# A two-block transformer step in fp32: early sums on TensorE, chunks handed out by name, scan states on VectorE

## The chip, the cores and the metric

One core of a Trainium2 chip runs the whole program. The metric is device time in microseconds (us), the median of the runs shown. Engine names are those of the profile: PE is TensorE's matmul, PEld its weight load, DVE VectorE, ACT ScalarE, POOL GpSimd, and SP the engine that issues the large DMAs.

## What is computed

One sequence of 256 tokens with 1024 features, all in fp32, goes through two blocks.

```python
# block 1: nine vectors of 1024 from a condition, then three residual steps
mod = silu(cond) @ w_mod + b_mod                    # w_mod is 1024 x 9216
x += 0.5 * g1 * swiglu(modulate(rms_norm(x), sh1, sc1))          # ffn1
b_gate, c_gate, v, u = split(modulate(rms_norm(x), sh2, sc2) @ w_in)
y_conv = b_gate * conv3(c_gate * v)                 # causal, width 3
y_ssm  = y * sigmoid(y @ glu_w + glu_b),  y = gelu(S5(u))        # complex linear scan
x += g2 * (concat(rms_norm(y_conv), rms_norm(y_ssm)) @ w_out)    # mixer
x += 0.5 * g3 * swiglu(modulate(rms_norm(x), sh3, sc3))          # ffn2
x  = rms_norm(x, final_norm)
# block 2: gated linear attention, squared-relu MLP, differential attention, MLP
h += gla(rms_norm(h));   h += mlp0(rms_norm(h))
h += diff_attention(...); h += mlp1(rms_norm(h))
```

## The kernel before

**Weights.** Every large product is written as three matmuls of rounded fp32 parts (`mm3`, L248): activation high by weight high, activation low by weight high, activation high by weight low. All weights come as 1 MB chunks of 128 x 2048 values, in the one order that `schedule()` writes down. The class `Stream` moves them: `load` issues a DMA on SP into one of three stage buffers (L141); `prep` makes the high part on ACT (`wh`, L170) and the low part on DVE (`wl`, L172), in halves of 128 x 1024, into one of four slots (five after the mixer); `take` hands the next chunk of the order to its user and prepares as many more as slots are free, unless `ahead` limits that; `free` gives slots back. A chunk in `locked` stops `prep`, and with it all that stands behind it in the order, stage buffers and DMAs included.

**Order.** The program writes each engine's instructions in the order in which the Python code runs; each engine runs its queue in order. An instruction that waits holds all behind it on its engine.

**The modulation vectors.** A chunk of `w_mod` isn't prepared: its four calls per group g are summed on DVE (`macc`, L839 and L841, one operation for each half chunk), and `mod_reduce` sums over the partitions with matmuls of a single column against `ones` (L862) and adds the bias on DVE (L866, L868). Groups 0 and 1 give shift and scale of ffn1 and are needed before its first matmul; groups 2 to 6 are spread over ffn1, group 7 over the mixer, group 8 over ffn2.

**A gated ffn** takes 11 steps s of 256 hidden features: up and gate products (`up`), a hidden tile with its high and low part (`hidh` on ACT L276, `hidl` on DVE L277), and the product down into four banks (`acc`). The first three steps have no down product yet, and their hidden parts are split when the fourth begins. The last three down products are the `tail`: their parts are mixed by `turn` with the norm of the token half 0 (`post`, `evac`) and the first token-major products of the next layer (`turn`). `side1` runs after each step of ffn1: due modulation sums and `ssm.step(s)`.

**The S5 scan.** `ssm.powers()` works out powers of the complex decay on POOL (L586 to L698, and one DVE reciprocal at L666); `step(2..4)` transposes them on PE (`s_end`), `readout()` and `tables()` go on on POOL, `step(8..10)` make `s_lag`. In the mixer `turning(j)` runs the scan of one half of the channels, with nine operations on DVE and five on POOL (L1124 to L1137); `conv_a`, `conv_v`, `conv_b` are the convolution.

**GLA** makes the decay of its six levels with `level_e` (POOL, L1348 and L1349) and `across_e` (POOL), `exp` on ACT, and `level_x` on DVE (L1359, L1361); `diagonal` (L1385) and `level_mm` (L1370) are the small matmuls; `ks` (L1447) is q times k.

Of the kernel before, what the change touches and what calls it, by code (L numbers as in the profile page):

```python
# [18 lines left out]
S = 256  # L19
# [13 lines left out]
MODS_FFN1 = (2, 3, 4, 5, 6)  # L33
MODS_MIXER = (7,)
# [21 lines left out]
def schedule():  # L56

# [33 lines left out]

    mods(range(2))
    ffn("ffn1", MODS_FFN1, 1)
    md = [4 * g + c for g in MODS_MIXER for c in range(4)]
    for c in (6, 7, 2, 4, 0, 3, 5, 1):
        w("w_in", c)
        if c in (0, 3, 5, 1):
            w("w_mod", md.pop(0))
# [13 lines left out]
    mlp(0)  # L112
    for name, j in DIFF_ORDER:
        w(name, j)
    for c in range(4):
        w("b_out", c)
    mlp(1)
    return it


class Stream:
# [23 lines left out]
    def prep(self, upto, items=10 ** 9):  # L145

        nc = self.nc
        while self.n_prep < min(items, len(self.items)):
# [9 lines left out]
            else:  # L158
                n = st.shape[-1]
                if key in self.special:  # L160
                    pool, th, tl = self.special[key]
                    self.used.append(None)
                    h, lo = (pool.tile([128, n], F32R, name=nm, tag=tg, bufs=1) for nm, tg in (("wh", th), ("wl", tl)))
                else:
                    pool, slot = self.slots.pop(0)
                    self.used.append((pool, slot))
                    h, lo = (pool.tile([128, n], F32R, name=nm, tag="%s%d" % (nm, slot), bufs=1) for nm in ("wh", "wl"))
                cuts = [(c, min(n, c + 1024)) for c in range(0, n, 1024)]
# [4 lines left out]
                self.ready[self.n_slot] = key, (h, lo)  # L173
# [11 lines left out]
    def take(self, name, j=0, ahead=10 ** 9):  # L185
        i = self.n_take
        self.n_take += 1
        self.prep(i + 1 + ahead)
        key, W = self.ready.pop(i)
        assert key == (name, j), (key, name, j)  # L190
        return W


class Net:
# [195 lines left out]
    def tail(self, acc, last, first, post, order=None):  # L390
# [23 lines left out]
    def turn(self, tail, evac, chunks, use):  # L414
# [5 lines left out]
        if tail is None:  # L420
            evac(0)
            evac(1)
        else:
# [12 lines left out]
            S.prep(S.n_take + n_c)  # L436
            tail.post(1)
            if self.after_tail is not None:
                self.after_tail()
                self.after_tail = None  # L440
                S.prep(S.n_take + n_c)
        Ws = []
        for i in range(2):
            for c in range(n_c):
# [7 lines left out]
                if i == 0 and c == 1 and n_c > 2:  # L452
# [21 lines left out]
    def ffn(self, tail, evac, ups, dn, steps, gated, post, side=None, n_first=3):  # L474
# [48 lines left out]
        for s in range(n_first, steps):  # L523
            res = []
            for u in ups:
                ps = self.bank_u("up")
                self.feat(self.take(u, s), self.hT, v3(ps, 2))
# [36 lines left out]
class Ssm:  # L564


    def __init__(self, N, p):
# [136 lines left out]
    def step(self, s):  # L704
# [3 lines left out]
        if 2 <= s <= 4:  # L708
            for b in ((0, 1), (2, 3, 4), (5, 6, 7))[s - 2]:
# [73 lines left out]
def build(N):  # L783
# [64 lines left out]
    def mod_reduce(g, new_bank, later=False):  # L848
# [15 lines left out]
        def finish():  # L864
            col = modf[:, 2 * blk + kind, :]
            nc.vector.tensor_tensor(out=col, in0=bank[:, 0:KD], in1=sv["b_mod"][:, g, :], op=ADD)  # L866
            if kind == 1:
                nc.vector.scalar_tensor_tensor(out=col, in0=col, scalar=1.0, in1=(G_FFN1, G_MIX, G_FFN2)[blk], op0=ADD, op1=MUL)  # L868

        if later:  # L870
            return finish
        finish()
# [21 lines left out]
    N.pad("pad_slots", 64)  # L894
# [40 lines left out]
    def side1(s):  # L935
        mods_ready(True)
        ssm.step(s)

    tail_places("ffn1_w_down", 10, 0)
    tail = N.ffn(None, lambda i: N.evac_mod(pts[i], i, modf[:, 1, :], modf[:, 0, :], N.hT),  # L940
                 ("ffn1_w_gate", "ffn1_w_up"), "ffn1_w_down", 11, True, post_ffn1, side1, 1)
# [4 lines left out]
        convw=sv["conv_w"], glub=sv["glu_b"], onorm=sv["out_norms"], ones=ones, xns=xns, mods=mods_ready))  # L946
# [87 lines left out]
def mixer(N, tail, evac, ssm, c):  # L1034
# [3 lines left out]
    vt, gt, act = nc.vector.tensor_tensor, nc.gpsimd.tensor_tensor, nc.scalar.activation  # L1038
# [66 lines left out]
    conv_v(0, vps)  # L1105
# [12 lines left out]
    def turning(h, m):  # L1118
# [775 lines left out]
```

## Time and profile before

| | us |
|---|---|
| median of 3 runs (1244.81 to 1246.57) | 1246.31 |
| the profiled execution's own time | 1243.52 |
| its span in the trace | 1241.8 |
| PE busy | 1140.0 |
| DVE busy | 796.8 |
| ACT busy | 613.7 |
| POOL busy | 237.1 |

Busy time is the sum over the whole span, the same for stages that wait for different things; where an engine waits is read from the waits and from timelines of single stages. PE's clock is shown as the share that the throttle granted (1.00 is 2.4 GHz, 0.50 is 1.2 GHz). Weights read from memory are 227.87 MB in all.

### The profile page before, as it was taken

The numbers are of one execution on the slowest core, as the hardware profiler recorded it, in microseconds if no ns is written. First come the engines' busy times: TensorE is split into PE (matmuls) and PEld (weight loads), VectorE is DVE, ScalarE is ACT, GpSimd is POOL, SyncE is SP. The second block draws the span as 40 slices with busy tenths as digits, with TensorE's granted clock in tenths as the row PEclk, the third lists the DMA queues.
The fourth block names the chain that finished last, engine by engine and source line by source line (L and its number), as shares of the span: only waits on it lengthen the run. The fifth ranks groups of instructions, "written<-read, shape, count | busy, mean of one in ns | idle before, by whom it ended". The sixth has DMA issues, their size and how long they took to land.

```text
span 1241.8 us, 18751 instructions
## 1 busy us (share of the span) xinstructions
PE 1140.0 (92%) x7780; PEld 1055.1 (85%) x7780; DVE 796.8 (64%) x934; ACT 613.7 (49%) x941; POOL 237.1 (19%) x304
## 2 busy tenths in 40 slices
PE   2689999989788899999697998999999899999998
PEld 2678998979777889997697988999989898899997
DVE  7698788677877855454567656544468776545441
ACT  3444443564265544444473656555456665645541
POOL 8994399401400000000214100000000000000000
PEclk9989999999789999999897999999999899899999
DMA  8598788436243765563144255556435333455540
GB/s 319 205 326 310 270 321 325 149 136 238 94 177 137 281 235 180 174 233 105 68 149 158 73 182 204 177 200 203 170 136 200 107 136 119 173 193 180 180 157 34
DMA packets 33093, 230.13 MB, mean 185 GB/s; under 512 B 3680, under 2 KB 4064, under 8 KB 5872
## 3 DMA queue, kind: packets, MB, share of 16 engines
q1 hardware_dynamic: 31536, 224.05, 50.5%
q10 hardware_dynamic: 1472, 4.88, 1.1%
q8 instruction: 61, 1.00, 0.3%
q14 instruction: 24, 0.20, 0.0%
HBM read 227.87 MB, written 1.05 MB: 184 GB/s over the span
## 4 chain that ended last, share of the span: by engine, by line
PE 68%; DVE 15%; ACT 7%; POOL 4%; DMA 3%; issue 3%; ACTq 0%; DVEq 0%; POOLq 0%
PE acc L248 27%; PE up L248 25%; PE turn L248 8%; DVE wl L172 7%; PE kqv L248 2%; ACT wh L170 2%; POOL s_small L612 1%; PE xnT L335 1%; POOL s_small L615 1%; DVE macc L841 1%; PE lev L1370 1%; DMA stage<-in_w 1%; DMA stage<-in_a_in 1%; ACT s_lag L734 1%; PE glu L248 1%
## 5 line engine op out<-in xcount | busy, mean ns | idle before, releaser
L172 DVE TENSOR_TENSOR wl<-stage,wh 128x1024 fp32r<-128x1024 f32 x351 | 429.5, 1270 | 144.2 <-ACT wh L170 144.2
L170 ACT CAST wh<-stage 128x1024 fp32r<-128x1024 f32 x351 | 347.2, 1044 | 147.1 <-PE acc L248 37.5
L248 PE MATMUL up<-hTh,wh 128*128 128x256 f32 x1024 | 288.1, 281 | 0.2 <-ACT s_end L715 0.2
L248 PE MATMUL up<-hTl,wh 128*128 128x256 f32 x1024 | 287.0, 280 | 0.0
L248 PE MATMUL up<-hTh,wl 128*128 128x256 f32 x1024 | 286.9, 280 | 0.0
L248 PEld LDWEIGHTS up<-hTh,wl 128*128 128x128 f32 x1024 | 195.4, 191 | 0.0
L248 PEld LDWEIGHTS up<-hTh,wh 128*128 128x128 f32 x1024 | 192.5, 188 | 2.4 <-ACT s_end L715 0.5
L248 PEld LDWEIGHTS up<-hTl,wh 128*128 128x128 f32 x1024 | 192.4, 188 | 1.6 <-issue 0.2
L248 PE MATMUL acc<-wh,hidh 128*128 128x512 f32 x288 | 116.6, 405 | 10.7 <-ACT hidh L276 5.4
L248 PE MATMUL acc<-wh,hidl 128*128 128x512 f32 x288 | 116.1, 403 | 9.8 <-DVE hidl L277 9.5
L248 PE MATMUL acc<-wl,hidh 128*128 128x512 f32 x288 | 115.6, 401 | 1.7 <-DVE wl L172 1.7
L248 PE MATMUL turn<-wh,hTh 128*128 128x256 f32 x320 | 92.4, 289 | 10.2 <-ACT hTh L276 10.2
L248 PE MATMUL turn<-wl,hTh 128*128 128x256 f32 x320 | 91.6, 286 | 1.7 <-DVE wl L172 1.7
L248 PE MATMUL acc<-wh,macc 128*128 128x512 f32 x288 | 93.1, 391 | 0.0
L248 PE MATMUL turn<-wh,hTl 128*128 128x256 f32 x320 | 91.9, 287 | 0.0
L841 DVE SCALAR_TENSOR_TENSOR macc<-stage,cact,macc 128x1024 f32<-128x1024 f32 x63 | 85.5, 1358 | 4.1 <-DMA stage<-in_w_mod 2.6
L248 PEld LDWEIGHTS acc<-wh,hidl 128*128 128x128 f32 x288 | 55.9, 194 | 24.1 <-DVE hidl L277 11.6
L248 PEld LDWEIGHTS acc<-wh,hidh 128*128 128x128 f32 x288 | 55.9, 194 | 23.5 <-ACT hidh L276 6.3
L248 PEld LDWEIGHTS turn<-wh,hTh 128*128 128x128 f32 x320 | 62.5, 195 | 11.0 <-ACT hTh L276 10.8
L248 PEld LDWEIGHTS acc<-wl,hidh 128*128 128x128 f32 x288 | 55.9, 194 | 13.7 <-DVE wl L172 3.1
L248 PEld LDWEIGHTS turn<-wl,hTh 128*128 128x128 f32 x320 | 62.5, 195 | 2.1 <-DVE wl L172 1.9
L248 PEld LDWEIGHTS acc<-wh,macc 128*128 128x128 f32 x288 | 54.1, 188 | 11.0
(401 smaller groups left out, 2023.4 us busy)
## 6 DMA issues: line engine op xcount, KB each, us to landing
stage<-in_w SPq DMA_DIRECT2D x64, 1024.0 KB, 4.8
stage<-in_w_mod SPq DMA_DIRECT2D x36, 1024.0 KB, 5.0
stage<-in_ffn_w_gate SPq DMA_DIRECT2D x22, 1024.0 KB, 4.8
stage<-in_ffn_w_up SPq DMA_DIRECT2D x22, 1024.0 KB, 4.8
stage<-in_ffn_w_down SPq DMA_DIRECT2D x22, 1024.0 KB, 4.8
stage<-in_a_in SPq DMA_DIRECT2D x12, 1024.0 KB, 5.1
stage<-in_w_in SPq DMA_DIRECT2D x8, 1024.0 KB, 5.1
stage<-in_w_kv SPq DMA_DIRECT2D x8, 1024.0 KB, 4.9
```

What stands on the lines that cost most here:

```text
L170: nc.scalar.copy(out=h[:, b:e], in_=st[:, b:e])
L172: nc.vector.tensor_tensor(out=lo[:, b:e], in0=st[:, b:e], in1=h[:, b:e].bitcast(F32), op=SUB)
L248: self.nc.tensor.matmul(out, lhs(l, k), rhs(r, k), start=first and n == 0, stop=last and n == 3 * n_k - 1)
L335: self.nc.tensor.transpose(out, src, self.ident)
L612: g.tensor_tensor(out=o, in0=x, in1=y, op=op)
L615: g.tensor_scalar(out=o, in0=x, scalar1=s1, scalar2=s2, op0=op0, op1=op1)
L734: nc.scalar.copy(out=self.lag[32 * i:32 * i + 32, 4 * b:4 * b + 4, 32 * i:128], in_=ks[:32, :, 0:128 - 32 * i])
L841: nc.vector.scalar_tensor_tensor(out=acc, in0=wv[:, k, :], scalar=cc, in1=acc, op0=MUL, op1=ADD)
L1370: nc.tensor.matmul(ps[:, 64 * e:64 * e + 64], ks[:, 128 * e:128 * e + 128], qs[:, 64 * e:64 * e + 64], start=True, stop=True)
```

## The change

Six parts, in the order of the program.

1. The chunks of modulation groups 0 and 1 are no longer summed on DVE. Each of the eight chunks goes straight to PE as 16 matmuls whose weights are 128 x 128 blocks of the chunk and whose moving operand is one column of the condition; `mod_early` adds the partial columns. The clearing of the scan's tables goes from POOL to DVE. The two `evac`s of ffn1's first turn now stand apart: after the first comes `St.prep(2)`, after the second, which follows the first token-major chunk, `ssm.powers()`.
2. Chunks are handed out by name. So a chunk can stand later in the order of the stream than in the order of use, and `swap` puts the locked last down chunk behind the two, three and three chunks that follow it. The first step of an ffn with a down product splits its first hidden parts before it prepares further chunks. `tail` puts both halves of hidden tile 0 first, and `turn` prepares one chunk, then two, then all.
3. Modulation group 7 (four chunks) moves from the mixer into ffn1. `s_end` comes one step later, `s_lag` one step earlier.
4. In the mixer, all of `turning` runs on DVE; `turning(0)` is queued ahead of `conv_v(0)`, `turning(1)` after `proj(5)`, and `outputs(0)` after three further products.
5. In GLA, `level_e` and `across_e` go from POOL to DVE, with two copies to ACT; the gate product stands between the halves of the first feature product; `a_z` has a place of its own; four `take`s prepare their followers later; `level_x` runs in pairs; the last gate chunk is split around `av`.
6. Four paddings change, so that the activation tile `hT` and others lie at other addresses.

```diff
-MODS_FFN1 = (2, 3, 4, 5, 6)
-MODS_MIXER = (7,)
+MODS_FFN1 = (2, 3, 4, 5, 6, 7)
...
     ffn("ffn1", MODS_FFN1, 1)
+    swap(2)
...
     ffn("ffn2", MODS_FFN2, 2)
+    swap(3)
...
     def take(self, name, j=0, ahead=10 ** 9):
-        i = self.n_take
         self.n_take += 1
-        self.prep(i + 1 + ahead)
-        key, W = self.ready.pop(i)
+        self.prep(self.n_take + ahead)
+        W, slot = self.ready.pop((name, j))
+        self.used.append(slot)
...
-        for f in range(2):
-            for n in range(n_l):
-                t.parts[0].append(part(0, n, f, first and n == 0, n == n_l - 1))
+        for n, f in [(0, 0), (0, 1)] + [(n, f) for f in range(2) for n in range(1, n_l)]:
+            t.parts[0].append(part(0, n, f, first and n == 0, n == n_l - 1))
...
-            for part in tail.parts[1][:early - 2]:
+            for part in tail.parts[1][:early]:
                 part()
-            S.prep(S.n_take + n_c)
-            for part in tail.parts[1][early - 2:early]:
-                part()
+            S.prep(S.n_take + 1)
             evac(0)
             for part in tail.parts[1][early:]:
                 part()
-            S.prep(S.n_take + n_c)
+            S.prep(S.n_take + 2)
             tail.post(1)
...
-                if i == 0 and c == 1 and n_c > 2:
+                if i == 0 and (c == 1 and n_c > 2 or c == 0 and tail is None):
                     evac(1)
...
-                self.feat(self.take(u, s), self.hT, v3(ps, 2))
+                begins = s == n_first and u == ups[0]
+                self.feat(self.take(u, s, 0 if begins else 10 ** 9), self.hT, v3(ps, 2))
...
-                if s == n_first and u == ups[0]:
+                if begins:
                     for b in range(n_first):
                         first_hid(b)
+                    self.S.prep(10 ** 9)
                     acc = self.acc_banks()
...
-        g.memset(p0, 0.0)
-        for c in range(2):
-            g.memset(self.out[c], 0.0)
-        g.memset(self.lag, 0.0)
+        for z in [p0] + self.out + [self.lag]:
+            N.nc.vector.memset(z, 0.0)
...
-        if 2 <= s <= 4:
+        if 3 <= s <= 5:
...
-        if 8 <= s <= 10:
+        if 7 <= s <= 9:
...
     def mod_part(g, c, st):
         wv = v3(st, 2)
+        if g < 2:
+            if c == 0:
+                early[g] = N.bank_a("mod")
+            for j in range(KD):
+                for k in range(2):
+                    nc.tensor.matmul(early[g][:, j * 8 + 2 * c + k:j * 8 + 2 * c + k + 1], wv[:, k, 128 * j:128 * j + 128],
+                                     cact[:, 2 * c + k:2 * c + k + 1], start=True, stop=True)
+            return
...
+    def mod_early(g):
+        tot = t([KD], "rs_sq", bufs=2)
+        nc.vector.tensor_reduce(out=tot, in_=v3(early[g][:, 0:64], KD), axis=AX.X, op=ADD)
+        col = modf[:, g, :]
+        nc.vector.tensor_tensor(out=col, in0=tot, in1=sv["b_mod"][:, g, :], op=ADD)
+        if g == 1:
+            nc.vector.scalar_tensor_tensor(out=col, in0=col, scalar=1.0, in1=G_FFN1, op0=ADD, op1=MUL)
...
-    St.prep(0, 4)
+    St.prep(0, 6)
     N.pad("pad_xn", 128)
     pts = [N.transp(N.normed(x[:, i, :])) for i in range(2)]
-    N.pad("pad_hT", 448)
+    N.pad("pad_hT", 256)
...
-    shift = mod_reduce(0, lambda: N.bank_a("mod"), True)
+    mod_early(0)
     St.prep(0)
-    shift()
     nc.sync.dma_start(out=bc, in_=a["ssm_bc"])
-    St.prep(1)
-    mod_reduce(1, lambda: N.bank_a("mod"))
-    ssm.powers()
+    mod_early(1)
...
+    def evac_first(i):
+        N.evac_mod(pts[i], i, modf[:, 1, :], modf[:, 0, :], N.hT)
+        if i == 0:
+            St.prep(2)
+        else:
+            ssm.powers()
...
     conv_a(0, ps)
-    conv_v(0, vps)
...
-        gt(out=m[0], in0=m[0], in1=m[1], op=ADD)
+        vt(out=m[0], in0=m[0], in1=m[1], op=ADD)
...
     turning(0, [t([512], "hm", bufs=2), t([512], "hm", bufs=2)] + pair(t([1024], "macc", bufs=2)))
-    turning(1, [t([512], "hidh1"), t([512], "hidl1")] + pair(t([1024], "macc", bufs=2)))
+    conv_v(0, vps)
     conv_b(0)
     conv_a(1, proj(3))
+    vps = proj(5)
+    turning(1, [t([512], "hidh1"), t([512], "hidl1")] + pair(t([1024], "macc", bufs=2)))
     outputs(0)
+    conv_v(1, vps)
     gelu(0)
-    conv_v(1, proj(5))
     conv_b(1)
     outputs(1)
...
-    c["mods"]()
     ps = sums(yq)
...
-        gt(out=ev[:, :, 1, :], in0=bv[:, :, 1, :], in1=ref, op=SUB)
-        gt(out=ev[:, :, 0, :], in0=ref, in1=bv[:, :, 0, :], op=SUB)
+        vt(out=ev[:, :, 1, :], in0=bv[:, :, 1, :], in1=ref, op=SUB)
+        vt(out=ev[:, :, 0, :], in0=ref, in1=bv[:, :, 0, :], op=SUB)
...
-    W = take("a_in", 7)
+    W = take("a_in", 7, 0)
     vt(out=kss[:, 2], in0=qf, in1=kf, op=MUL)
     level_x(0)
+    level_x(1)
     level_e(2)
     exp(Es[2])
-    level_x(1)
     level_e(3)
     exp(Es[3])
+    N.S.prep(10 ** 9)
```

## Rows read from the trace of the kernel before

**Rows 1.** Page, busy time of the engines with its share of the span.

```profile
PE 1140.0 (92%) x7780; PEld 1055.1 (85%) x7780; DVE 796.8 (64%) x934; ACT 613.7 (49%) x941; POOL 237.1 (19%) x304
```

**Rows 2.** Waits of PE: waiting tile, releaser, total us, times, longest us.

```profile
PE xnT L335 <- POOL s_small L612: 22.6, 1, 22.6
PE turn L248 <- ACT hTh L276: 10.2, 2, 6.3
PE xnT L335 <- DVE xn L980: 9.9, 2, 9.0
PE acc L248 <- DVE hidl L277: 9.5, 4, 5.0
PE diag L1385 <- DVE ks L1447: 7.1, 1, 7.1
PE y L1154 <- DVE xn L1136: 6.0, 1, 6.0
PE acc L248 <- ACT hidh L276: 5.4, 3, 2.6
PE acc L248 <- ACT s_tab L281: 5.3, 1, 5.3
PE acc L248 <- ACT wh L170: 5.0, 2, 3.8
```

**Rows 3.** Timeline of PE: start, us, instructions, [idle before <-releaser].

```profile
26.08 3.41 PE L862 MATMUL mod<-ones,macc 128*128 128x1 f32 x16
33.90 3.57 PE L862 MATMUL mod<-ones,macc 128*128 128x1 f32 x16 [4.41 <-DVE macc L841]
43.75 0.58 PE L248 MATMUL turn<-wh,hTh 128*128 128x256 f32 x1 [6.28 <-ACT hTh L276]
...
139.58 1.84 PE L862 MATMUL mod<-ones,macc 128*128 128x1 f32 x16
```

**Rows 4.** Timelines of DVE and POOL, opening and the scan's powers.

```profile
6.26 6.39 DVE L839 TENSOR_SCALAR macc<-stage,cact 128x1024 f32<-128x1024 f32 x1 [6.26 <-DMA stage<-in_w_mod]
...
41.60 0.25 DVE L666 RECIPROCAL s_small<-s_small 128x16 f32<-128x16 f32 x1 [3.72 <-POOL s_small L612]
...
92.75 5.04 POOL L698 COPY s_out<-s_tab 64x256 f32<-64x256 f32 x4
...
142.96 0.40 POOL L754 TENSOR_SCALAR s_out<-s_tab 64x256 f32<-64x256 f32 x1 [19.55 <-PE s_end L335]
```

**Rows 5.** Windows: sum; PE, PEld, DVE, ACT, POOL busy; PEclk, DMA share, GB/s.

```profile
78.44:85.47 7.03, 7.03 (x24) 5.70 (x25) 6.31 (x6) 1.38 (x3) 6.83 (x7) 0.73 0.95 318
85.47:244.50 159.03, 158.79 (x1186) 148.91 (x1184) 129.58 (x119) 69.10 (x91) 107.06 (x121) 1.00 0.75 274
...
62.20:84.00 21.80, 16.40 (x109) 14.68 (x108) 21.24 (x17) 8.03 (x10) 21.28 (x16) 0.84 0.97 340
...
662.40:672.70 10.30, 10.30 (x49) 10.30 (x49) 6.81 (x6) 3.94 (x6) 5.67 (x4) 0.50 0.29 118
```

**Rows 6.** Timelines of POOL and DVE in the mixer.

```profile
308.58 1.29 POOL L1126 TENSOR_TENSOR hm<-hm 128x512 f32<-128x512 f32 x1 [16.13 <-DVE hm L1125]
...
309.90 2.30 DVE L1130 TENSOR_TENSOR_SCAN hm<-s_tab,hm 128x512 f32<-128x512 f32 x1 [0.27 <-POOL hm L1126]
312.24 0.69 DVE L1131 TENSOR_TENSOR xn<-hm,s_tab 128x512 f32<-128x512 f32 x1
...
330.82 2.60 DVE L841 SCALAR_TENSOR_TENSOR macc<-stage,cact,macc 128x1024 f32<-128x1024 f32 x2
```

**Rows 7.** Timeline of DVE, ffn2's first down product.

```profile
430.93 2.60 DVE L841 SCALAR_TENSOR_TENSOR macc<-stage,cact,macc 128x1024 f32<-128x1024 f32 x2
433.45 1.28 DVE L277 TENSOR_TENSOR hidl<-hidT,hidh 128x512 fp32r<-128x512 f32 x2
```

**Rows 8.** Timelines of SP and DVE, end of ffn2 and GLA.

```profile
548.91 28.79 SPq L141 DMA_DIRECT2D stage<-in_a_in  x3
...
574.99 6.90 DVE L172 TENSOR_TENSOR wl<-stage,wh 128x1024 fp32r<-128x1024 f32 x6 [1.66 <-ACT wh L170]
...
646.26 7.14 DVE L172 TENSOR_TENSOR wl<-stage,wh 128x1024 fp32r<-128x1024 f32 x4
```

More of the change, by code (lines that the diff above doesn't have):

```diff
@@ L90, in mlp, with swap, settle @@
             w("w2_%d" % l, n)
+    def swap(n):
+        behind.append((len(it) + n, it[-1]))
+    def settle():
+        for at, item in behind:
+            it.remove(item)
+            it.insert(at - 1, item)
+    behind = []
     mods(range(2))
     ffn("ffn1", MODS_FFN1, 1)
-    md = [4 * g + c for g in MODS_MIXER for c in range(4)]
+    swap(2)
     for c in (6, 7, 2, 4, 0, 3, 5, 1):
         w("w_in", c)
-        if c in (0, 3, 5, 1):
-            w("w_mod", md.pop(0))
     w("w_out", 0)
@@ L549, in ffn @@
                 side(s)
+        last = [(hd, self.take(dn, steps - 3 + n)) for n, hd in enumerate(pend)]
         if gated:
             nc.scalar.preload_act_table(AF.Sqrt)
-        last = [(hd, self.take(dn, steps - 3 + n)) for n, hd in enumerate(pend)]
         self.acc = acc
@@ L862, in mod_reduce @@
             nc.tensor.matmul(bank[:, k:k + 1], acc[:, 128 * k:128 * k + 128], ones[:, 0:1], start=True, stop=True)
[L864 to L872, printed above, removed]
+        col = modf[:, 2 * blk + kind, :]
+        nc.vector.tensor_tensor(out=col, in0=bank[:, 0:KD], in1=sv["b_mod"][:, g, :], op=ADD)
+        if kind == 1:
+            nc.vector.scalar_tensor_tensor(out=col, in0=col, scalar=1.0, in1=(None, G_MIX, G_FFN2)[blk], op0=ADD, op1=MUL)
     todo = list(range(2, 9))
@@ L1298, in gla @@
     nc.gpsimd.memset(step01.rearrange("p (n c) -> p n c", c=64)[:, :, 0:1], 0.0)
-    wz = [v3(w, KD) for w in take("a_z")]
+    wz = [v3(w, KD) for w in take("a_z", 0, 0)]
     zp = N.bank_u("z")[:16, :S]
@@ L1306, in gla, with featb, gates @@
     nc.vector.tensor_copy(out=zT[:16], in_=zp)
-    def featb(ch, dst, scale):
-        ps = N.bank_u("qk")
-        N.feat(take("a_in", ch), N.hT, v3(ps, 2))
+    def featb(ch, dst, scale, between=None, ahead=10 ** 9):
+        pv = v3(N.bank_u("qk"), 2)
+        W = take("a_in", ch, ahead)
+        wv = [v3(w, KD) for w in W]
+        for k in range(2):
+            cs = slice(128 * k, 128 * k + 128)
+            N.mm3(pv[:, k, :], lambda l, kk: wv[l][:, kk, cs], lambda r, kk: N.hT[r][:, kk, :], KD)
+            if k == 0 and between is not None:
+                between()
         N.S.free()
-        act(out=flat(dst), in_=ps, func=AF.Copy, scale=scale)
+        act(out=flat(dst), in_=flat(pv), func=AF.Copy, scale=scale)
     qT, kT = t2([4, S], "qT"), t2([4, S], "kT")
-    featb(0, qT[:, 0:2, :], 128 ** -0.5)
     gp = []
-    for h2 in range(2):
-        ps = N.bank_a("gate")
-        for k in range(2):
-            h = 2 * h2 + k
-            nc.tensor.matmul(ps[:, S * k:S * k + S], wgu[:16, 128 * h:128 * h + 128], zT[:16, :], start=True, stop=True)
-        gp.append(ps)
+    def gates():
+        for h2 in range(2):
+            ps = N.bank_a("gate")
+            for k in range(2):
+                h = 2 * h2 + k
+                nc.tensor.matmul(ps[:, S * k:S * k + S], wgu[:16, 128 * h:128 * h + 128], zT[:16, :], start=True, stop=True)
+            gp.append(ps)
+    featb(0, qT[:, 0:2, :], 128 ** -0.5, gates, 0)
     e1, mn = t2([4, S], "E", bufs=2), t2([4, S], "E", bufs=2)
@@ L1462, in gate_chunk @@
         tok_chunk(8 + hd, [sg[hd][:, i, :] for i in range(2)], W)
-    W = take("a_in", 8)
+    W = take("a_in", 8, 0)
     level_x(2)
+    level_x(3)
     level_e(4)
     exp(Es[4])
-    level_x(3)
     level_e(5)
     exp(Es[5])
+    N.S.prep(10 ** 9)
     gate_chunk(0, W)
@@ L1479, in gla @@
         exp(E)
+    N.S.prep(10 ** 9)
     gate_chunk(1, W)
@@ L1486, in gla @@
     across()
+    W = take("a_in", 11)
+    last_gate = N.bank_u("vg")
+    N.tokm(W, N.hT, 0, last_gate[:, :CW])
     for hd in range(3):
@@ L1522, in gla @@
     nc.scalar.preload_act_table(AF.Silu)
-    W = take("a_in", 11)
-    ps = N.bank_u("vg")
-    for i in range(2):
-        N.tokm(W, N.hT, i, ps[:, CW * i:CW * i + CW])
-    N.S.free()
-    act(out=flat(sg[3]), in_=ps, func=AF.Silu)
+    act(out=flat(sg[3]), in_=last_gate, func=AF.Silu)
     c["load"]("m0", t([D], "macc", bufs=2))
```

69 lines of the change are left out of this document (36 added, 33 removed).

## The prediction

> **What bounds the kernel now.** I read the busy times first: PE works 92% of the span [rows 1], so the end is PE's own work plus what it waits for, and any edit must be followed to one of these two. Then the waits of PE by who ends them [rows 2]: the reader is to see that few are large, and that nearly all lie at the joints between layers. The opening has 22.6 us before the first transpose; the other eight rows are joints and sum to 58.4 us. Behind a wait the clock falls: the first down product of ffn1 ran 7.03 us at a mean clock of 0.73 [rows 5], so at full clock it would be 7.03 x 0.73 = 5.1 us. I take that difference, 1.9 us, as the price of one fall. Then the timelines of the joints, to see what stands ahead of the releaser on its own queue [rows 3, 4, 6 to 8]. Last the windows, for the load on DMA [rows 5].
>
> **Part 1, the opening: later.** Before, the eight chunks of groups 0 and 1 are summed on DVE as they land, and PE adds 16 matmuls for each group, 3.41 and 3.57 us [rows 3]; the first product starts at 43.75 [rows 3]. After, PE does 32 matmuls for each chunk. Their form (128x128 weights, one column) is that of the row, whose price is 3.41 / 16 = 0.213 us there and 1.84 / 16 = 0.115 us later, at 139.58 [rows 3]. Which holds? The stretch 662.40 to 672.70 is full of matmuls of one and of 64 columns, PE is busy all of its 10.30 us, and the granted clock stays 0.50 [rows 5]: such matmuls didn't raise it. So I take 0.213: 8 x 32 x 0.213 = 54.5 us, and 16 transposes at the same price 3.4 us. PE can begin when the first chunk has landed, 6.26 [rows 4], so it ends near 64.2. The new sums on DVE, the modulated tile, its split on ACT and the first weights follow; the old path took 43.75 - 37.47 = 6.3 us from the last 128x1 matmul [rows 3], of which DVE stood 3.72 us behind a reciprocal that waited for POOL [rows 4]; that is out of the way now, but the first weights are prepared only behind the first `evac`, so 5 to 6 us remain and the first product comes at 69 to 70, 26 us later. Some returns. DVE no longer sums, so wl and hidl are not behind it; the weights are staged while PE sums; the acc wait for hidl (5.0, the longest [rows 2]) and its fall (1.9) go, and about 3.5 us of waits for weights in the first three steps, where DMA ran at a share of 0.97 [rows 5]. Together 10.5: **+15.5 us** (+13 if more of the DMA bound is worked off, +24 if nearly nothing returns).
>
> The Trainium skill, "TensorE: Matmul & The Clock Gate", section "Why this matters for your kernels", tells one to keep TensorE continuously busy to get its full clock. By that rule 55 us of unbroken sums would run at 2.4 GHz. The row of 662.40 to 672.70 speaks against it for matmuls this narrow; the rival below has its time.
>
> **Parts 1 and 3, ffn1's body.** Before, 159.03 us with PE busy 158.79 [rows 5], for eight steps. Group 7's reduction comes in at 1.8 us [rows 3] and leaves the mixer, where I count it out. Its four chunks bring the stream to 8 x 3 + 24 = 48 items; PE needs (159.0 + 1.8) / 48 = 3.35 us for each. At the 340 GB/s of the full stretch [rows 5] an item of 1.049 MB takes 3.08 us. That is near enough that some steps wait: +1.5 (0 to +6). The powers on POOL begin after the second `evac`; they ran 41.6 to 97.8 before [rows 4], 56 us, so now from about 74 to 130, while `s_end`, queued on PE one step later, comes near 136. The readout then begins some 17 us after the old 142.96 [rows 4] and `s_lag` a step earlier; a wait there would hold PE, 0 to 4 us, inside the same range. **+3.3 us** with the reduction.
>
> **Part 2, the joints.** End of ffn1: acc waited 3.8 us for wh [rows 2], behind a table load on ACT; now the takes come first, but wl still follows: **-2.5** (0 to -3.8). Start of ffn2: macc (2.60) stands ahead of hidl (1.28) on DVE [rows 7], and acc waits for hidl; with the splits first, about 3 of the 4.5 us that the three shorter hidl waits share [rows 2] and a fall go, less 0.4: **-4.5**. The starts of mlp0 and mlp1 wait for hidh, 5.4 us in three, the longest 2.6 [rows 2]: **-2.3**, and with a fall 2.6 + 1.9 = **-4.5**. End of ffn2: the locked last down chunk holds the stream, three issues on SP last 28.79 us, and then six wl halves come in one run, 6.90 us, just before the final norm [rows 8]; xnT waits 9.0 [rows 2], the tail's acc 1.2 for wh (5.0 - 3.8), and there are two falls: 14.0 us in all. A chain of adds, norm and scale remains in any case, which I put at 8: **-6** (-2 to -10). Preparing one chunk, then two, then all makes the third chunk late at three turns: **+1.5** (0 to +5).
>
> **Part 4, the mixer.** `turning` on DVE is 12 operations at 0.69 and two scans at up to 2.30 [rows 6], at most 12.9 us, and no handovers to POOL (1.29 and more each [rows 6]). Queued ahead of conv_v, and without two half sums (2.60 [rows 6]) of group 7 ahead of it, it ends some 7 us earlier. y waited 6.0 us for its last result [rows 2]: 5 go. The convolution pays: conv_v(0) is now behind 12.9 us of DVE and conv_b waits for it; PE has three more products in front of y to cover this. Two falls (3.8) go; of the 5.3 us wait for s_tab [rows 2] only 1, since conv_b(1) stays last; the first hTh of ffn2 waited 10.2 - 6.3 = 3.9 [rows 2], with part of a fall 4.7; the reduction takes out 1.8. Sum 5 + 3.8 + 1 + 4.7 + 1.8: **-16.3** (-8 to -20; at -8 conv_b and the wl behind `turning` are the new last).
>
> **Part 5, GLA.** diag waited 7.1 us for ks, behind wl [rows 2]; with prep after it, 7.1 and a fall go, 9.0. But the levels add 0.69 each to DVE [rows 6], and four wl halves (7.14 [rows 8]) still stand behind the scan while the next feature product needs one: +4. **-5** (-12 to +3; above zero if the later wl holds the gate chunk).
>
> **Part 6, addresses.** No row shows an effect of an address; 1024 `up` matmuls of each kind run alike. 0 (-5 to +5).
>
> **Sum.** 15.5 + 3.3 - 2.5 - 4.5 - 2.3 - 4.5 - 6 + 1.5 - 16.3 - 5 = **-20.8 us**. The profiled execution took 1243.52 (span 1241.8), so it becomes 1222.7; from the median, 2.8 above, **1225.5**.
>
> **Rivals.** (a) *The sums run warm.* For: PE is busy without a break. Against: rows 5 as above. At 0.115 us the sums save 8 x 32 x 0.098 = 25 us: about **1200**. 5%. (b) *Slower: the stream starves ffn1.* Three stage buffers, 48 items, and each transfer waits for the buffer's reader on ACT and DVE, or now PE. For: the body's mean was 274 GB/s, 3.83 us an item [rows 5]. Against: PE was never starved there, so 274 is what was asked for, and 340 has been shown. Each 0.1 us of pace above 3.35 costs 4.8 us; with the 1.5 already counted it decides at 3.35 + 22.3 / 48 = 3.8 us an item. At 4.0 it costs 31.2 - 1.5 = 29.7: **1255**. 10%. (c) *The reorders only shift the waits.* wh and wl keep their total, and each joint has another operand nearly as late; the later gains, 39.6 after the 1.5, come half: **1245**. For: the wl runs of rows 8 are as long as before. Against: the waits of rows 2 have different, named releasers. 13%, of which 6 within, 5 faster, 2 slower.
>
> **How the numbers follow.** The forecast has 72%, nearly all faster. A measurement of this kernel can tell about 0.2% (2.5 us) from no change. Faster: 72 + 5 + 5, less 1 for its upper tail, 0.81; same 0.06; slower 0.13, of which 10 from (b), 2 from (c), 1 from the forecast. The terms' ends don't fall together; added in squares, upward 8.5, 4.5, 5, 8, 8, 5, 4 give some 17, downward about 13. The range reaches down to 1203, just above (a), and up to 1247, past (c); left out are (a), most of (b) and tails, under 2 in 10.
>
> **What would show it.** PE's sums at 0.213 us each and a clock of 0.50 up to the first product near 69; ffn1's down product starting near 95 without a 5 us wait; DMA near 340 GB/s and PE without gaps in ffn1's body; no y wait above 1 us; diag's wait gone and a new one of some 4 us at the feature product behind the scan; xnT after ffn2 waiting 3 to 5 us in place of 9.0. It is wrong if the first product starts before 55 (clock), if ffn1's body shows stage waits above 6 us in sum (stream), or if rows 2 return with other releasers (rival c).

## The result and the profile after

The changed kernel takes 1254.61 us (median of 4 runs, 1253.14 to 1255.67) against 1245.56 before: a ratio of 1.0073, 95% interval [1.0055, 1.009], so 9 us slower. The forecast was 1225.5 us, faster. The profiled execution took 1254.78 us, its span is 1253.1.

The page of the kernel after, busy times:

```profile
PE 1189.5 (95%) x8004; PEld 1105.8 (88%) x8004; DVE 782.0 (62%) x951; ACT 613.7 (49%) x944; POOL 171.4 (14%) x270
```

PE is busy 49.5 us more than before [rows 1], while the end comes 11.3 us later: work was put on PE, and waits were taken off. The waits of PE after:

```profile
PE xnT L345 <- DVE xn L1005: 8.1, 2, 7.3
PE mod L845 <- DMA stage<-in_w_mod: 7.1, 1, 7.1
PE acc L258 <- ACT s_tab L291: 5.2, 1, 5.2
PE s_end L345 <- DVE hidf L472: 5.1, 1, 5.1
PE qk L258 <- ACT wh L181: 4.8, 1, 4.8
...
PE acc L258 <- ACT wh L181: 4.1, 1, 4.1
PE up L258 <- DVE hidf L472: 3.8, 2, 2.0
...
PE up L258 <- ACT s_end L722: 1.8, 1, 1.8
PE qk L258 <- DVE wl L183: 1.6, 1, 1.6
...
PE diag L1419 <- DVE ks L1481: 1.0, 1, 1.0
```

The 22.6 us of the opening, the waits for hidl, hidh and for y are gone [rows 2], and diag's fell from 7.1 to 1.0. New are the first sums' 7.1 us for their first chunk, s_end and up behind hidf, and qk behind wh.

The opening, PE's timeline after:

```profile
7.11 41.09 PE L845 MATMUL mod<-cact,stage 128*128 128x1 f32 x192 [7.11 <-DMA stage<-in_w_mod]
...
48.06 3.65 PE L345 MATMUL xnT<-ident,xn 128*128 128x128 f32 x16
...
69.45 0.58 PE L258 MATMUL turn<-wh,hTh 128*128 128x256 f32 x1 [4.29 <-ACT wh L181]
```

The first 192 sums cost 41.09 / 192 = 0.214 us each, as in the slower of the two rows of before [rows 3], and the first product starts at 69.45.

Where the 11.3 us lie, stage by stage, from the two timelines of PE (from the start of one stage's first matmul to the next's, in us):

| stage | before | after | moved | forecast |
|---|---|---|---|---|
| start to the end of ffn1's first down product | 85.5 | 101.1 | +15.6 | +15.5 |
| ffn1's body, to its tail | 159.0 | 179.6 | +20.6 | +3.3 |
| ffn1's tail, to the mixer's first product | 24.3 | 25.4 | +1.1 | -2.5 |
| mixer, to ffn2's first product | 124.2 | 107.8 | -16.4 | -16.3 |
| ffn2's start, to its second pair of `up` | 47.8 | 43.1 | -4.7 | -4.5 |
| ffn2's body | 130.3 | 132.1 | +1.8 | 0 |
| ffn2's tail, to GLA's first product | 32.2 | 26.2 | -6.0 | -6 |
| GLA, to its output product | 110.3 | 115.2 | +4.9 | -5 |
| mlp0 | 205.6 | 204.8 | -0.8 | -2.3 |
| differential attention | 150.8 | 150.2 | -0.6 | 0 |
| mlp1 | 168.2 | 164.0 | -4.2 | -4.5 |

The forecast column leaves out the +1.5 for three turns, which belongs to no single row. Eight of the eleven came within 2 us of the forecast. Three didn't: ffn1's body, by 17.3 us, GLA, by 9.9, and ffn1's tail, by 3.6.

### The profile page after: what moved, and what is told of

It reads as the page before. It is cut to its first block, busy times and chain, and to the rows that moved or that the text cites. A ratio compares the mean times of both kernels' runs of the same rounds, so it can differ in the third digit from the quotient of the medians.

```text
span 1253.1 us, 19179 instructions
## 1 busy us (share of the span) xinstructions
PE 1189.5 (95%) x8004; PEld 1105.8 (88%) x8004; DVE 782.0 (62%) x951; ACT 613.7 (49%) x944; POOL 171.4 (14%) x270
## 4 chain that ended last, share of the span: by engine, by line
PE 69%; DVE 16%; ACT 8%; DMA 3%; issue 3%; ACTq 0%; SPq 0%; DVEq 0%
PE acc L258 24%; PE up L258 24%; PE turn L258 8%; DVE wl L183 7%; PE mod L845 4%; PE kqv L258 3%; ACT wh L181 3%; DVE macc L859 2%; DMA stage<-in_w_mod 1%; PE xnT L345 1%; DMA stage<-in_ffn_w_up 1%; DMA stage<-in_a_in 1%; PE s L1720 1%; ACT s_lag L741 1%; PE qk L258 0%
## 5 line engine op out<-in xcount | busy, mean ns | idle before, releaser
L183 DVE TENSOR_TENSOR wl<-stage,wh 128x1024 fp32r<-128x1024 f32 x351 | 423.8, 1255 | 131.0 <-ACT wh L181 130.6
L258 PE MATMUL up<-hTh,wh 128*128 128x256 f32 x1024 | 292.4, 286 | 7.1 <-DVE hidf L472 3.8
L258 PE MATMUL up<-hTl,wh 128*128 128x256 f32 x1024 | 290.6, 284 | 0.0
L258 PE MATMUL up<-hTh,wl 128*128 128x256 f32 x1024 | 290.6, 284 | 0.0
L258 PEld LDWEIGHTS up<-hTh,wh 128*128 128x128 f32 x1024 | 197.3, 193 | 11.3 <-DVE hidf L472 4.2
L258 PEld LDWEIGHTS up<-hTl,wh 128*128 128x128 f32 x1024 | 197.3, 193 | 1.7 <-issue 0.5
L258 PE MATMUL acc<-wh,hidl 128*128 128x512 f32 x288 | 113.5, 394 | 0.0
L859 DVE SCALAR_TENSOR_TENSOR macc<-stage,cact,macc 128x1024 f32<-128x1024 f32 x49 | 69.1, 1410 | 2.2 <-DMA stage<-in_w_mod 1.1
L258 PEld LDWEIGHTS acc<-wh,hidl 128*128 128x128 f32 x288 | 54.8, 190 | 12.8 <-DVE hidl L287 0.9
L258 PEld LDWEIGHTS acc<-wl,hidh 128*128 128x128 f32 x288 | 54.8, 190 | 11.8 <-DVE wl L183 1.8
```

What stands on the lines that cost most here:

```text
L183: nc.vector.tensor_tensor(out=lo[:, b:e], in0=st[:, b:e], in1=h[:, b:e].bitcast(F32), op=SUB)
L258: self.nc.tensor.matmul(out, lhs(l, k), rhs(r, k), start=first and n == 0, stop=last and n == 3 * n_k - 1)
L859: nc.vector.scalar_tensor_tensor(out=acc, in0=wv[:, k, :], scalar=cc, in1=acc, op0=MUL, op1=ADD)
```

## Experiments

Each ratio is to the kernel before, measured beside it (median 1243.95 to 1244.53 us, against 1245.56 beside the changed kernel). Where two runs of different chips are set against each other, each is taken as its distance from the kernel before beside it; for the changed kernel that is +9.1 us.

### Addresses

The first difference that the traces show runs through all stages. Ends of three excerpts of PE's timeline: thirteen products of 256 columns after, then eleven and ten before:

```profile
499.75 0.28 PE L258 MATMUL up<-hTh,wh 128*128 128x256 f32 x1
...
501.19 0.28 PE L258 MATMUL up<-hTh,wh 128*128 128x256 f32 x1
```

```profile
499.76 0.28 PE L248 MATMUL up<-hTh,wh 128*128 128x256 f32 x1
...
500.94 0.28 PE L248 MATMUL up<-hTl,wh 128*128 128x256 f32 x1
```

```profile
301.78 0.28 PE L248 MATMUL proj<-hTh,wh 128*128 128x256 f32 x1
...
302.80 0.28 PE L248 MATMUL proj<-hTh,wh 128*128 128x256 f32 x1
```

After, 1.44 us for 12 steps: 120.0 ns from start to start. Before, 1.18 us for 10 steps, some 118 ns, and 1.02 us for 9, 113.3. By the middle step of each group of 48 such products, 106 of 107 groups have 120.0 ns after; before, 26 of 109 have some 113.3 and 82 some 117.8. By the paddings, modulo 512 bytes, hT stands 448 above the weight slots before, 256 after; no trace shows an address. Two kernels exchange the paddings alone.

**e1, the kernel before with the new paddings.**

```diff
-    N.pad("pad_hT", 448)
+    N.pad("pad_hT", 256)
-    N.pad("pad_slots", 64)
+    N.pad("pad_slots", 256)
-            N.pad("pad_hq", 448, N.pool2)
+            N.pad("pad_hq", 128, N.pool2)
-                N.pad("pad_tail", 128, N.pool2)
+                N.pad("pad_tail", 448, N.pool2)
```

> The kernel before with the four paddings alone changed (hT lies 192 bytes lower; nothing else moves against the weight slots). Theory A, addresses: in the trace of the changed kernel all 112 groups of 48 products of 256 columns start 120.0 ns apart, before 113.3 (28 groups) or 117.8 (83). If the address does it, this kernel shows 120.0 everywhere: 28 x 48 x 6.7 ns + 83 x 48 x 2.2 ns = 17.8 us later, 1263 us. Theory B, other edits (the load on DVE, the order): 113.3 and 117.8 stay and the time is 1246, the same.

1251.28 us, ratio 1.0065 [1.0044, 1.0085]; 120.0 ns in 108 groups.

```profile
PE 1152.9 (92%) x7780; PEld 1067.7 (85%) x7780; DVE 796.1 (64%) x934; ACT 614.0 (49%) x941; POOL 240.1 (19%) x304
```

The paddings set the step, as theory A said, and PE's busy time grows by 12.9 us. The time grows only by 6.8, far less than the 17.8 expected: the waits for hidl, diag and y shrink (9.5 to 8.3, 7.1 to 5.9, 6.0 to 5.0 us), for a slower PE reaches its waits later.

**e2, the changed kernel with the old paddings** (the same diff, reversed).

> The changed kernel with the four paddings of before. Theory A, addresses: products 113.3 or 117.8 ns apart again, 17.8 us off, 1254.6 - 17.8 = 1237 us. Theory B: 120.0 stays, 1254.6.

1244.41 us, ratio 1.0014 [0.9999, 1.0029]: from 9.1 us above the kernel before to 0.1 below, 9.2 us off, with some 113.3 or 117.8 ns back in 105 of 107 groups. In its trace 3.1 us of that are no matter of the step: its last 64 sums took 10.5 us in place of 13.7 (see e8). So the two kernels together put the paddings at about +7 us, most of the distance to the kernel before, but not of that to the forecast.

### First sums

**e3, part 1 undone in the changed kernel.**

```diff
         if tail is None:
             evac(0)
+            evac(1)
...
-        for z in [p0] + self.out + [self.lag]:
-            N.nc.vector.memset(z, 0.0)
+        g.memset(p0, 0.0)
...
-        if g < 2:
-            if c == 0:
-                early[g] = N.bank_a("mod")
...
-            return
...
-    St.prep(0, 6)
+    St.prep(0, 4)
...
-    mod_early(0)
+    shift = mod_reduce(0, lambda: N.bank_a("mod"), True)
     St.prep(0)
+    shift()
...
-    mod_early(1)
+    St.prep(1)
+    mod_reduce(1, lambda: N.bank_a("mod"))
+    ssm.powers()
...
-        if i == 0:
-            St.prep(2)
-        else:
-            ssm.powers()
```

> The changed kernel with part 1 undone (groups 0 and 1 summed on DVE, powers ahead of the first evac, both evacs together, tables cleared on POOL), all else as changed. Theory: ffn1's first down product ends near 85 in place of 101, and POOL's powers run 25 us earlier beside the first steps, so ffn1's body loses less to DVE: 15.5 to 20 us off, 1235 to 1239. Rival, the later start of the weight stream only shifts the same DMA bound: ffn1's body grows by what the opening gains, 1250 to 1255.

1228.29 us, ratio 0.9873 [0.9847, 0.9898]: 25.3 us off (from 9.1 above the kernel before to 16.2 below), more than expected. Windows, the first down product and ffn1's body (columns as in rows 5):

```profile
72.77:78.40 5.63, 5.63 (x28) 4.67 (x27) 5.59 (x5) 2.04 (x3) 5.47 (x5) 1.00 0.90 330
78.40:254.94 176.54, 166.76 (x1202) 155.95 (x1200) 142.91 (x135) 71.42 (x96) 107.33 (x129) 0.97 0.77 284
```

The down product ends at 78.40, without a wait and at full clock: 22.7 us ahead of the changed kernel and 7.1 ahead of the kernel before [rows 5]. So the wait for hidl and the fall of the clock go without part 1 too. Of the parts that are left, part 2 is the one that edits this joint, by splitting the first hidden parts earlier; it was not run by itself. ffn1's body is 176.5 us even so, 17.5 more than before: 3.1 of the 20.6 us go with part 1, and neither the sums nor the later start of POOL's powers makes the rest.

**e8, the sums with a warm start**, products of ones ahead of them while PE has nothing to do.

```diff
+    wb = N.bank_u("warm")
+    for j in range(22):
+        nc.tensor.matmul(wb[:, 0:128], ones[:, 0:128], ones[:, 0:128], start=True, stop=True)
     N.pad("pad_macc", 384)
```

> The changed kernel with 22 products of 128 columns of ones against ones put ahead of the first sums, while PE has nothing to do. Their result is not used. Theory: the sums don't hold the clock: after a few us they go back to 0.213 us each, and the time is that of the changed kernel less at most 4 us: 1251 to 1255. Rival, the sums only lacked a start: they run at 0.115 us, 256 x 0.098 = 25 us less on PE, then DMA (8 chunks at 3.1 us) bounds the opening: 1229 to 1232.

1247.85 us, ratio 1.0039 [1.0021, 1.0057]: 5.2 us less than the changed kernel, where the theory had at most 4. Windows of e8, the warm start and the first 192 sums (8.50 to 45.87):

```profile
5.62:12.44 6.82, 6.82 (x63) 6.82 (x63) 3.49 (x2) 0.00 (x0) 5.07 (x24) 1.00 1.02 429
12.44:49.99 37.55, 37.55 (x179) 37.55 (x178) 2.48 (x8) 6.09 (x14) 5.05 (x24) 0.50 0.49 175
...
20.00:32.00 12.00, 12.00 (x58) 12.00 (x57) 0.19 (x1) 0.37 (x1) 0.00 (x0) 0.50 0.47 169
...
49.20:54.00 4.80, 4.80 (x39) 4.80 (x39) 0.00 (x0) 0.00 (x0) 0.00 (x0) 0.86 0.15 63
```

A window of the changed kernel, and the last 64 sums there and in e8:

```profile
20.00:32.00 12.00, 12.00 (x58) 12.00 (x58) 0.38 (x1) 0.56 (x1) 0.00 (x0) 1.00 0.49 176
...
51.51 13.65 PE L845 MATMUL mod<-cact,stage 128*128 128x1 f32 x64
...
49.17 10.54 PE L845 MATMUL mod<-cact,stage 128*128 128x1 f32 x64
```

The 1.00 in the changed kernel's window is no reading, since no clock had been recorded yet: 58 sums in 12 us are the same there as in e8 at 0.50. With a warm start, the granted clock stood at 1.00 up to 12.44 us and fell back to 0.50 while PE was busy every moment. So the first 192 sums gained 3.7 us (37.4 in place of 41.1, begun 1.4 later) and no more: the sums don't hold the clock, and rival (a) isn't borne out. A further 3.1 us come from the last 64 sums, behind the 16 transposes: the clock was at 1.00 for 3.4 us there in e8 (50.0 to 53.4) and in e2 (51.6 to 55.0), which has no warm start. In the changed kernel's trace those sums ran at 0.213 us throughout. What decides between the two is open.

### ffn1's body

DVE and SP after, the first two modulation chunks that come one behind the other:

```profile
122.54 5.65 DVE L859 SCALAR_TENSOR_TENSOR macc<-stage,cact,macc 128x1024 f32<-128x1024 f32 x4
128.11 0.68 DVE L472 TENSOR_TENSOR hidf<-up,act 128x512 f32<-128x512 f32 x1
...
115.07 2.92 SPq L152 DMA_DIRECT2D stage<-in_w_mod  x2
```

24 chunks in place of 20 mean three per step in steps 3 to 6, and the stream has the second and the third one after the other. The four half sums of such a pair stand on DVE ahead of hidf, which frees the banks that PE's next `up` and `s_end` wait for. (In ffn1 only one step, not three, runs ahead of the first down product; in ffn2 two.) The chain that ended last, in this stage: all but about 1% on PE before, from 85.5 to 215; after, it leaves PE, here ahead of the longest wait, 5.1 us at s_end:

```profile
by line: PE up L248 60.8%; PE acc L248 29.5%; PE mod L857 2.7%; PE mod L862 2.6%; PE s_end L335 2.4%; PE s_lag L725 1.5%; ACT s_end L715 0.5%; ACT hm L728 0.5%; issue 0.1%
```

```profile
156.19 1.21 DVE macc L859
157.42 1.30 DVE macc L859
158.74 6.90 DMA stage<-in_w_mod
...
165.74 0.76 DVE macc L857
166.52 1.28 DVE macc L859
167.81 0.61 DVE hidf L472
```

So hidf stands behind a half sum, the half sum behind the landing of its chunk, and that transfer was issued only when an earlier half sum had freed a stage buffer. Queue and stream are links of one chain. The first test takes group 7 out, the second only moves the third chunk.

**e4, group 7 back in the mixer.**

```diff
-MODS_FFN1 = (2, 3, 4, 5, 6, 7)
+MODS_FFN1 = (2, 3, 4, 5, 6)
+MODS_MIXER = (7,)
...
         w("w_in", c)
+        if c in (0, 3, 5, 1):
+            w("w_mod", md.pop(0))
...
     conv_part(0, 1)
+    c["mods"]()
     ps = sums(yq)
```

> The changed kernel with modulation group 7 back in the mixer's chunks. Theory: the 12 us of waits of PE between 119 and 172 come from hidf queued on DVE behind the third half sums of a step; with 20 chunks in place of 24 half of them go (-6), the reduction moves (0), and the mixer's DVE queue grows by 10.4 us of sums, of which some 3 reach PE: -3, 1251. Rival, the waits come from DVE's slower operations beside POOL's powers: they stay, and the mixer's 3 to 8 us come on top, 1258 to 1262.

1256.79 us, ratio 1.0111 [1.0085, 1.0136]: 12.3 us above the kernel before, 3.2 more than the changed kernel, a miss of both. ffn1's body is 8.7 us shorter (100.6 to 271.6), but the mixer pays more, 120.6 us in place of 107.8:

```profile
PE y L1182 <- DVE xn L1164: 8.9, 1, 8.9
...
PE s_end L349 <- DVE hidf L476: 2.8, 1, 2.8
```

So moving group 7 out of the mixer is worth a few us more than it costs. And ffn1's chunks stand here in the order of the kernel before, no third one in any step, yet 5.6 of the 12.1 us of waits in the body stay (2.8 here, 1.8 at up for s_end, 1.0 at up for act), and the body is 11.9 us longer than before. The third chunks aren't the whole cause.

**e5, part 1 undone and the old paddings**, the neighbour for what follows.

> The changed kernel with part 1 undone and the four paddings of before. If the two costs add: 1254.6 - 26.3 (sums) - 10.2 (paddings) = 1218 us. If the paddings' gain is partly waiting that the other edit had made, as the 6.8 us of the paddings alone suggest: 1221 to 1224.

1220.85 us, ratio 0.9819 [0.9799, 0.9838]: 23.1 us below the kernel before, 6.9 more than e3. The costs add, but for some 2 us.

**e6, the third chunk behind the down chunk** (on e5).

```diff
-            if s > 2 and len(md) > 2 * (10 - s):
-                w("w_mod", md.pop(0))
             if s - first < 8:
                 w(pre + "_w_down", s - first)
+            if s > 2 and len(md) > 2 * (10 - s):
+                w("w_mod", md.pop(0))
```

> The kernel of the run beside it (part 1 undone, paddings of before) with one more edit: where a step of ffn1 has a third modulation chunk, it stands behind the step's down chunk in the stream, no longer behind the second one and so no longer ahead of hidf on DVE. The number of chunks is the same. Theory Q, a queue: PE's waits in ffn1's body, about 10 us, come from hidf behind two chunks' half sums, so most go: -7 to -10 us against its neighbour. Rival S, the stream: six chunks a step at 3.05 us are 18.3 us against 17.2 us of PE work, and they stay so in any order: 0 to -2 us.

1214.88 us, ratio 0.9768 [0.9746, 0.9789]: 6.0 us off, with the same chunks and bytes. DVE of e6, where one chunk's half sums are left ahead of hidf, and the chain that ended last, from 76 to 175 us:

```profile
115.74 0.74 DVE L852 TENSOR_SCALAR macc<-stage,cact 128x1024 f32<-128x1024 f32 x1
116.52 1.28 DVE L854 SCALAR_TENSOR_TENSOR macc<-stage,cact,macc 128x1024 f32<-128x1024 f32 x1
117.72 0.68 DVE L473 TENSOR_TENSOR hidf<-up,act 128x512 f32<-128x512 f32 x1
```

```profile
by line: DVE wl L183 25.5%; DMA stage<-in_ffn_w_up 24.5%; issue 17.9%; DVE macc L854 16.0%; ACT wh L181 10.7%; DVE hidf L473 3.5%; DVE macc L852 1.4%; DVE gate L879 1.3%; ACT xn L286 0.5%; ACTq L847 0.3%; ACT hidh L286 0.2%; ACTq L181 0.2%;
```

The waits of up for hidf (3.1 us in e5) are gone, and s_end's fell from 6.0 to 3.6; up's wait for act rose from 0.2 to 1.4. That is nearer to theory Q than to S, but short of Q's 7 to 10: 7.3 us of waits stay, and the chain still runs through DVE and the transfers of `up` chunks, without a product of PE in it.

### The end of ffn2, and GLA

**e7, GLA as before** (on e5; the function `gla` of the kernel before, and this line):

```diff
-    St.special["a_z", 0] = N.sb, "azh", "azl"
```

> The same neighbour with part 5 undone (the GLA function as before; levels on POOL). The prediction gave part 5 -5 us; the trace has the stretch from GLA's first token-major product to its output product 4.9 us longer than before. Theory: part 5 itself lost, since the new waits for wh and wl (4.8 and 1.6 us at qk) outweigh diag's: this run is 3 to 6 us faster than its neighbour. Rival: the stretch is longer because of addresses and of the split last gate chunk, and part 5 gains: 3 to 6 us slower.

1209.56 us, ratio 0.9728 [0.971, 0.9746]: 11.3 us off. The spans of the two traces differ by 9.5 us, of which only 1.8 lie in GLA (115.3 to 113.5 us) and 8.2 just ahead of it. DVE before the final norm, the changed kernel and then e7:

```profile
591.57 4.83 DVE L183 TENSOR_TENSOR wl<-stage,wh 128x1024 fp32r<-128x1024 f32 x5 [0.26 <-ACT wh L181]
600.02 2.36 DVE L183 TENSOR_TENSOR wl<-stage,wh 128x1024 fp32r<-128x1024 f32 x2 [3.62 <-ACT wh L181]
602.30 0.68 DVE L394 SCALAR_TENSOR_TENSOR act<-acc,gate 128x512 f32<-128x512 f32 x1
```

```profile
560.33 4.83 DVE L183 TENSOR_TENSOR wl<-stage,wh 128x1024 fp32r<-128x1024 f32 x5 [0.26 <-ACT wh L181]
565.08 0.68 DVE L394 SCALAR_TENSOR_TENSOR act<-acc,gate 128x512 f32<-128x512 f32 x1
```

In the changed kernel a further chunk is prepared between the run of wl and the residual add; DVE waits 3.62 us for its wh and works 2.36 us, and xnT comes that much later (a wait of 7.3 us there and 7.1 in e5, 1.2 in e7).

**e9, a_z in a slot** (on e6: the line above alone).

> The kernel with the third modulation chunk behind the down chunk (1214.9 us), with one line less: a_z has no place of its own and takes a slot again. Theory: with its own place the stream no longer stops at a_z before the final norm, so more wh and wl halves stand ahead of the norm on ACT and DVE; without it xnT's wait after ffn2, 7.0 us, falls to about 1 as it did with the whole of GLA as before: -6 to -8 us, 1207 to 1209. Rival: the wait fell there for another reason (the takes of GLA), and this run is the same, 1214 to 1216.

1210.99 us, ratio 0.9729 [0.9711, 0.9747]: 4.0 us less than e6, about half of the theory's 6 to 8. The wait of xnT fell from 7.0 to 1.2 us, as the theory said; the price is in GLA (117.6 us, 113.3 in e6), where the chunk behind a_z now waits for a slot:

```profile
PE qk L258 <- ACT wh L181: 10.6, 1, 10.6
```

In e6 that wait was 5.2; a wait of vg, 0.2 in e6, is 3.6 here. So the place for a_z trades one wait for another, and loses by it.

**e10, e6 with GLA as before.**

> Part 1 undone, paddings and GLA of before, third modulation chunk behind the down chunk: the two gains add to 1220.9 - 6.0 - 11.3 = 1203.6 us, and against the run beside it this tells what GLA's own reordering is worth without a_z's place: 3 to 5 us if the waits for wh and wl at qk (5.2 and 1.6) are a loss, 0 if diag's wait takes their place.

1205.61 us, ratio 0.9691 [0.9676, 0.9706]. This beats both kernels: 38.5 us less than before. Against e9 on the same chip, 5.4 us of it come from GLA's own order. There diag waits again for ks, but qk no longer:

```profile
PE diag L1408 <- DVE ks L1470: 5.5, 1, 5.5
```

**e11 and e12, hT at two more distances** (on e10): 128 and 64 above the weight slots modulo 512.

```diff
-    N.pad("pad_hT", 448)
+    N.pad("pad_hT", 128)
-    N.pad("pad_slots", 64)
+    N.pad("pad_slots", 384)
```

> The run beside it with hT 320 bytes lower (modulo 512 it stands 128 above the weight slots; 448 in the kernel before, 256 in the changed one). Theory A: the distance modulo 512 sets how far apart the products start; each distance has its own step, so the trace shows one value, not the mixture of 113.3 and 117.8 ns. 113.3 everywhere would be some 8 us less PE time and 4 to 6 us less in all; 120.0 as at 256, 6 to 10 us more.

> As the run beside it, with hT 64 above the weight slots modulo 512. If the sign of the distance doesn't matter, it is as at 448 (64 below): 113.3 and 117.8 ns mixed and the same time within 3 us. If it does, another single step.

At 128: 1213.2 us, ratio 0.9752 [0.973, 0.9774], 7.6 us more than e10, with steps of 119 to 120 ns in 101 of 109 groups. At 64: 1207.07, ratio 0.97 [0.9676, 0.9724], and 113.3 and 117.8 ns mixed, as at 448. So 64 above is like 64 below, and both are better than 128 or 256. In all these kernels the two paddings add to 512, so hT moves while the slots stay: whether the distance counts or hT's own place was not tested. What sets 113.3 or 117.8 in one kernel stays open too: in the kernel before, `up` in ffn2's body has some 117.8 throughout, while its first two groups and `proj` in the mixer have some 113.3, with the same hT and the same slots.

## Why the prediction failed

The arithmetic of the opening held where it was read: the sums at 0.214 us, the first product at 69.45 and the down product's end at 101.08 (forecast 69 to 70 and some 101). The mixer, the starts of ffn2 and mlp1 and the tail of ffn2 came out as forecast, within a microsecond, though not always for the reasons given. Four steps failed. Of the signs that the prediction named, two show the same: PE had gaps of 12.1 us in ffn1's body, and xnT after ffn2 waited 7.3 us, not 3 to 5.

1. **ffn1's body, +3.3 against +20.6.** The step that failed is the stream's term, +1.5 with a bound of 6 us. I judged it by rates, 3.08 us for the bytes of an item against 3.35 us of PE time. The question missed is the one that I had asked of the mixer: what stands ahead of the operand on its queue. In the trace after, PE's waits there sum to 12.1 us, nearly all for banks that hidf frees or for s_end; some 2.0 go to the clock that falls behind them (13.8 us for the 96 products at 171.5, 11.8 for others), 3.2 to the addresses (e1's body), 1.8 to the reduction, 19.1 in all. e6 shows that the third chunk's place in the queue, with the load unchanged, is worth 6.0 us, and e4 that four chunks fewer are worth 8.7, the reduction's 1.8 among them. Taking from the 11.9 us that e4's body keeps the 3.2 of the addresses and the 3.1 of part 1 (e3) leaves, if they add, some 5.6 us that no run isolates: neither part 2 nor the later step of `s_end` was undone by itself. Rival (b) has the stage and half of the mechanism: DMA moved 349 GB/s at its fullest, and a transfer that waited for its buffer's reader on DVE stands in the chain, but what PE waited for was the queue of DVE behind it. That (b)'s 1255 us is what was measured is luck: it leaves all other terms as forecast, and the pace was 179.6 / 48 = 3.7 us an item, not 4.0.
2. **Addresses, 0 (-5 to +5) against about +7.** I wrote that no row shows an effect of an address, which was true and no bound: the two steps of 113.3 and 117.8 ns were there in the timelines, unexplained, and some 5,200 products at 6.7 or 2.2 ns are 17 us of PE time. The effect is spread over the stages: it is why ffn2's body, with no edit in it, is 1.8 us longer (e1 has the same 1.8).
3. **GLA, -5 against +4.9.** The wait of diag fell by 6.0 us and its products took 1.6 less, 7.7 of the 9 forecast. The step that failed is the price of the new wait at qk, +4: the wait was 6.4, and the products behind it ran at a lower clock.

```profile
642.17:672.43 30.26, 23.80 (x171) 23.30 (x171) 17.63 (x18) 19.03 (x22) 0.00 (x0) 0.83 0.37 135
```

   At 120 ns each its 168 products would take 20.2 us, so the place cost 10.1. New waits at a and vg add 1.8. Not priced at all was a_z's own place, which lets the stream run one chunk further just ahead of the final norm: ffn2's tail still gained its 6 us, but e9 shows that this line cost a wait of 5.8 us there. e7's GLA, with the old order, takes 113.5 us against 110.3 before because the granted clock was 0.50 for 24.0 us of it, in three stretches, against 17.1; in e12, with the same order, it was 17.1 again and GLA took 109.8.
4. **ffn1's tail, -2.5 against +1.1.** The table load did move behind the casts of wh, but acc's wait for wh stayed, 3.8 us before and 4.1 after.

Three terms were right by number and wrong by reason. I credited part 1 with 10.5 us that return at the first down product. e3 has 7.1 us of them, the wait for hidl and the fall, without part 1; only some 3 are its own. So part 1 as a whole costs 25 us, and the +15.5 is 22.7 less the gain of another part. It didn't move the forecast, but it would have misled anyone who takes the change apart: undoing part 1 alone is worth 25 us.

The mixer's -16.3 against -16.4 rests on group 7 more than on part 4. With group 7 back (e4), 12.8 of the 16.4 us are back too: the first y doesn't wait, but the second does, 8.9 us. I had priced its leaving at 1.8 and a share of y's 5. Offsetting this, a fall of the clock was worth far more than 1.9 here. The first 48 products of y, before and after:

```profile
311.30:328.36 17.06, 10.67 (x51) 10.34 (x50) 16.73 (x15) 0.00 (x0) 13.34 (x8) 0.59 0.00 0
...
356.92:362.38 5.46, 5.46 (x51) 5.46 (x50) 5.39 (x9) 0.00 (x0) 0.00 (x0) 1.00 0.94 378
```

They took 10.7 us behind the wait, against 5.5: a price of 5.2. And acc's wait for s_tab, of which 1 us was to go, stayed at 5.2. Last, of the -6 at ffn2's tail only 1.7 came from xnT's wait; 4.3 came from the tail's products ahead of it, 18.3 us before, with 2.1 of waits and a lower clock, and 13.9 after.

Of the clock, the Trainium skill, "TensorE: Matmul & The Clock Gate", "Why this matters for your kernels", says that keeping TensorE busy gives the full clock. By that rule the 41 us of unbroken sums would have run at 2.4 GHz; they ran at half, and e8 shows them losing a clock they were given. For these sums the measurement decides. The same page of the Trainium skill, "Back-to-back issue gap", gives 256 / 2.4 + 2.5 = 109 ns, an estimate by its formula, for a single warm product of 256 columns. It says that in a stream of weight loads and products the two together set the spacing. In this case's streams the step was 113.3, 117.8 or 120.0 ns, and it changed when only paddings changed.

## What to carry to other kernels

When work is added to an engine that isn't the bound, don't compare rates alone; list what now stands ahead of the operand that frees PE's banks. Four added chunks cost 8.7 us in ffn1 and would have cost 12.8 in the mixer, and moving the third chunk of a step alone gave 6.0. A line that gives a tile a place of its own can also move later preparation forward, into whatever critical chain comes next. A wait is not the whole price where the clock falls behind it: here that added between 1.6 and 5.2 us. And an unexplained spread in the step of like instructions is a cost that a change of addresses can move: measure it before calling it zero.

## What was unexpected of the hardware

- Matmuls of 128 x 128 weights by one column, without a gap for 41 us, ran at 0.214 us each. After a warm start (e8), the granted clock fell from 2.4 to 1.2 GHz at 12.4 us and stayed there to 50.0 with PE always busy; then it stood at 2.4 GHz for 3.4 us, and fell again under the last sums.
- Products of 256 columns start 113.3 or 117.8 ns apart when the moving tile lies, by the paddings, 64 bytes above or below the weights modulo 512, 119 to 120 at 128, and 120.0 at 256. The better address was worth 6.8 us on the kernel before, 9.2 on the changed kernel (3.1 of them, in its trace, from the clock in the opening), and 7.6 on e10 against e11.
